# The indexer's second products on 128 rows instead of 64, with zeros in the other half, in a hybrid encoder step

## The chip, the core and the metric

The kernel runs on one core of a Trainium2 chip. The metric is the device time of one execution in microseconds (us); less is better. The engines are PE (TensorE: the products, with PEld for its weight loads), DVE (VectorE), ACT (ScalarE), POOL (GpSimd) and SP (SyncE, which here only issues transfers).

## The reference, cut to what matters

One layer mixes 512 prompt tokens and 64 sample tokens with a gated DeltaNet branch and a sparse attention branch. The sparse attention first needs a score for each pair of query and key, from 16 indexer heads of 64 dimensions that share one set of keys, and keeps the best keys of each query:

```python
dots = jnp.einsum('bthd,bsd->bths', qi.astype(jnp.float32), KI.astype(jnp.float32))
score = jnp.einsum('bth,bths->bts', wi.astype(jnp.float32), jax.nn.relu(dots))
visible = (k_pos[None, :] // CHUNK) <= (q_pos[:, None] // CHUNK)
score = jnp.where(visible[None], score, -jnp.inf)
top_val, top_idx = lax.top_k(score, topk)
```

For the prompt the keys are those of the prompt itself (512), for the sample they are 1024 cached ones and 64 new ones.

## The kernel before

**Products in parts.** Nearly all matrix products are made in the type fp32r, with each factor written as a first part (its rounding to fp32r) and a second part (what is left). A product is the sum of three: first by first, first by second, second by first. For the weight products these are the names `hh`, `hl` (the two parts of the input) and `whi`, `wlo` (the two parts of a weight tile).

**The stream of weight tiles.** `run_tile` takes one tile of 128 output columns after another: 96 products of 128 rows by 288 columns, first the 64 with `whi`, then the 32 with `wlo`. Within a tile it has ACT split the next tile's weights (hook 4, 14, 24, 34) and SP load a later one (hook 84). Everything else is made by small generators, called tasks. After each product `self.tick()` steps the tasks whose due time has come by a planner's own clock, and so each engine's instructions get one fixed order when the program is built.

**The scores.** Eight tiles of the stream, `qi0` to `qi7`, give the indexer's queries, two heads each. `qi_epi` writes for each of the two heads `s` a tile `qi[:, s, :]` of 128 rows: the head's first part in one half of the rows (rows 0 to 63 for s = 0, rows 64 to 127 for s = 1) and its second part in the other half. The keys' first part stands twice in `kih`, in both halves of the rows, and the keys' second part twice in `kil`. So one product of `qi` with `kih` over all 128 rows gives first by first and second by first at once, and a second product gives first by second from the 64 rows that hold the query's first part alone. `score` makes, for each of the two heads, three such pairs for the query blocks t = 3, 2, 1 (with 512, 384 and 256 keys), and then three units for the sample, each of three products with all 128 rows (`qss` with `kih`, `kih` and `kil`, 364 or 362 keys). Here a unit is what goes into one PSUM tile `dot`: two products for the prompt, three for the sample. There are two `dot` banks; ACT takes each unit out with a Relu (`relu`), and DVE adds it to the score (`msk`, `msks`).

**Where this lies.** `misc` splits the keys when its weight tile is done, `cache_idx` does so for the cached keys, and `run` allots `kih`, `kil` and zeroes the two `qss` tiles. The units of one pair of heads lie among the next weight tile's products. When the eighth pair is done, the choice of the best keys runs on DVE, and the stream goes on with the next weight tiles.

Of the kernel before, what the change touches and what calls it, by code (L numbers as in the profile page):

```python
# [7 lines left out]
F32 = mybir.dt.float32  # L8
F32R = mybir.dt.float32r
I32 = mybir.dt.int32  # L10
AF = mybir.ActivationFunctionType
ALU = mybir.AluOpType
# [6 lines left out]
TP = 512  # L19
# [186 lines left out]
class Kern(Plan):  # L206
# [446 lines left out]
    def misc(self):  # L653
        i, o, p, A, V, G, mT = self.i, self.o, self.p1, self.A, self.V, self.G, self.mT
# [3 lines left out]
        for a, b, at in ((0, TP, 0), (TP, T, TP + PAST)):  # L658
            c = slice(at, at + b - a)
            A.activation(self.kih[0:64, c], mT[0:64, a:b], AF.Copy)  # L660
            A.activation(self.kih[64:128, c], mT[0:64, a:b], AF.Copy)
            for R in (slice(0, 64), slice(64, 128)):
                V.tensor_tensor(self.kil[R, c], mT[0:64, a:b], self.kih[0:64, c].bitcast(F32), op=ALU.subtract)
        mt = p.tile([128, 5, 112], F32, name="mt", bufs=1)
        G.memset(mt[64:128, 4, :], 0.0)
        pt = yield from self.tr("mtp")
# [25 lines left out]
        x = p.tile(sh, F32, name="sx", bufs=1)  # L692
# [104 lines left out]
    def qi_epi(self, m):  # L797
        def epi(ps, s):
# [7 lines left out]
            halves = slice(0, 64), slice(64, 128)  # L806
            for b, R in enumerate(halves):
                A.activation(q[R, b, c], ps[R, :n], AF.Copy)
                V.tensor_tensor(q[halves[1 - b], b, c], ps[R, :n], q[R, b, c].bitcast(F32), op=ALU.subtract)
            if s:  # L810
                qs = self.qss[m % 2]
                for R in halves:
                    self.two(ps[R, 224:288], qs[R, 0, R], qs[R, 1, R])
# [3 lines left out]
    def score(self, m, qi, qs):  # L817
        p, A = self.p1, self.A
        accs, acs = self.msk, self.msks
        if m:  # L820
            yield from self.wait(self.score_tasks[m - 1])
        else:
            yield from self.wait(self.misc_task, self.cache_task)
        units = []
        for s in range(2):
            R = slice(64 * s, 64 * s + 64)
            for t in (3, 2, 1):
                nk = 128 * t + 128
                q, k = qi[:, s, 128 * t:128 * t + 128], slice(0, nk)
                units.append((((q, self.kih[:, k]), (q[R], self.kil[R, k])), nk, accs[t],  # L830
                              self.wi[:, t, 2 * m + s:2 * m + s + 1], m == 0 and s == 0))
        for a, n in ((0, 364), (364, 362), (726, 362)):
            kh, kl = (k[:, TP + a:TP + a + n] for k in (self.kih, self.kil))
            units.append((((qs[:, 0, :], kh), (qs[:, 1, :], kh), (qs[:, 0, :], kl)), n, acs[:, a:a + n],
                          self.wis[:, m:m + 1], m == 0))
        yield [qi, qs]
        last = []
        for n, (parts, w, acc, sc, first) in enumerate(units):
            if len(last) >= 2:
                yield [last[-2]]  # L840
            pd = yield from self.tp(f"dot{m}_{n}")
            for x, (q, k) in enumerate(parts):
                self.mm(pd[:, :w], q, k, start=x == 0, stop=x == len(parts) - 1)
            r = p.tile([128, 512], F32, tag="relu", name=f"relu{m}_{n}")
            A.activation(r[:, :w], pd[:, :w], AF.Relu)
            if first:
                self.V.tensor_scalar(acc, r[:, :w], sc, None, op0=ALU.mult)
            else:
                self.V.scalar_tensor_tensor(acc, r[:, :w], sc, acc, op0=ALU.mult, op1=ALU.add)
            last.append(r)  # L850
        if m == 7:
            yield from self.topk_all()
            self.topk_task = self.spawn(self.topks())
# [935 lines left out]
    def run(self):  # L1789
        tc = self.tc  # L1790
        with ExitStack() as ctx:
            ctx.enter_context(tc.manual_schedule())
            self.consts(ctx)
            cp = self.cp
            self.wi = cp.tile([128, 4, 16], F32, name="wi")
            self.wis = cp.tile([128, 8], F32, name="wis")
            for n in ("beta", "gc", "egc", "kds"):
                setattr(self, n, cp.tile([128, 5, 16], F32, name=n))
            self.gate = cp.tile([128, KO, 2], F32, name="gate")
            self.diag = cp.tile([128, 64], F32, name="diag")  # L1800
            self.heads, self.att, self.kvT, self.tok = {}, {}, {}, {}
            self.score_tasks, self.topk_task = [], None
            self.topk_gap, self.solve_gap, self.gada_gap = 100, 0, 5000
            self.plan()
            self.hctx = ExitStack()
            pss = self.start(ctx, self.hctx)
            self.catt, self.ap = self.pool("att", bufs=1)
            self.msk = [self.ap.tile([128, 128 * t + 128], F32, name=f"msk{t}") for t in range(4)]
            self.msks = self.ap.tile([128, NS], F32, name="msks")
            self.c1, self.p1 = self.pool("p1")  # L1810
            self.gpool, self.p2 = lambda: self.p1, None
            p = self.p1
            self.kih, self.kil = (p.tile([128, TP + NS], F32R, name=n, bufs=1) for n in ("kih", "kil"))
            self.qss = []
            for b in range(2):
                q = p.tile([128, 2, 128], F32R, name=f"qss{b}", bufs=1)
                self.V.tensor_scalar(q, self.ident.unsqueeze(1).to_broadcast([128, 2, 128]), 0.0, None, op0=ALU.mult)
                self.qss.append(q)
            self.tri = p.tile([128, 2, 128], F32, name="tri", bufs=1)
            self.cache_task = self.spawn(self.cache_idx())  # L1820
            self.load(3)
            for n in range(2):
                for s in range(2):
                    self.stream[n]["epi"](pss[2 * n + s], s)
            self.S.dma_start(self.tri, self.i["k_tri"])
            self.load(4)
            for n in range(2, len(self.stream) - 2):
                self.run_tile(n)
            self.run_last(n + 1)
            self.drain()  # L1830
            for _ in self.finish((2, 3, 4)):
                pass
            for c in (self.c8, self.c6, self.cmg, ):
                c.close()
# [57 lines left out]
```

## Time and profile before

| what | value |
|---|---|
| time, median of 3 runs | 3108.05 us (3101.53 to 3108.31) |
| the profiled execution: its time | 3106.55 us |
| its span, first to last instruction | 3104.8 us |
| PE busy | 2972.8 us, 96% of the span |
| DVE, ACT, POOL busy | 1389.1, 1542.5, 390.0 us |
| first and last product of the scores (`dot`) | 189.4 us, 328.2 us |

The time of an execution is the span and some 1.75 us around it. An engine's products are pipelined: a product's row shows how long it is in the engine, and the distance from its start to the next one's start shows what it costs when products follow each other without a pause. The granted clock of PE is given as a share of 2.4 GHz (0.5 is 1.2 GHz).

### The profile page before, as it was taken

What the parts mean: (1) busy time and instruction counts of PE and PEld (TensorE: products, weight loads), DVE (VectorE), ACT (ScalarE), POOL (GpSimd) and SP (SyncE); (2) the same over time, 40 slices, a digit from 0 to 9 for tenths busy, and PEclk for the clock granted to TensorE, in tenths of its full rate; (3) what the DMA queues carried; (4) which work ended last, traced back from release to release, by engine and by line L of the source; (5) the groups of instructions that cost most, each with busy time, mean ns of one, the idle gap of its engine ahead of it and who ended that gap; (6) DMA issues with size and microseconds to landing.
All of it is one profiled execution on the core that took longest, in us unless ns stands there. A gap on an engine that the chain in (4) does not pass through costs nothing.

```text
span 3104.8 us, 56419 instructions
## 1 busy us (share of the span) xinstructions
PE 2972.8 (96%) x22363; PEld 2816.3 (91%) x22363; DVE 1389.1 (45%) x4057; ACT 1542.5 (50%) x3332; POOL 390.0 (13%) x727
## 2 busy tenths in 40 slices
PE   6999999999999999999998799999999899999997
PEld 2588999999989989999998699999999899999897
DVE  3334899566667657765651244334422111111112
ACT  3255444555555556665653345444544444444454
POOL 1010111111111111111110000101101111111110
PEclk8999999999999999999999899999999999999999
DMA  9865787766666666676767767776769899888875
GB/s 325 270 147 114 171 185 175 159 162 161 154 144 145 150 145 146 145 167 136 165 153 159 163 160 168 188 177 158 175 148 248 227 234 232 213 209 214 225 159 141
DMA packets 567242, 552.40 MB, mean 178 GB/s; under 512 B 53505, under 2 KB 466066, under 8 KB 565762
## 3 DMA queue, kind: packets, MB, share of 16 engines
q1 hardware_dynamic: 512690, 351.58, 40.1%
q0 software_dynamic: 54144, 197.16, 33.5%
q8 instruction: 176, 2.88, 0.4%
q14 instruction: 88, 0.72, 0.1%
q10 hardware_dynamic: 144, 0.07, 0.0%
HBM read 303.54 MB, written 48.04 MB: 113 GB/s over the span
## 4 chain that ended last, share of the span: by engine, by line
PE 49%; DMA 9%; SPq 3%; ACT 2%; DVE 2%; issue 1%; POOL 0%; ACTq 0%; DVEq 0%; POOLq 0%
PE mm L218 41%; SPq L55 3%; DMA gbl<-d_gb 2%; DMA za<-d_za 2%; DMA wlo<-wraw 2%; PE ob L218 1%; PE lg L218 1%; DMA xf<-in_x_sample 1%; ACT wlo L55 1%; ACT whi L55 1%; PE po L218 1%; PE pT L233 1%; PE obs L218 1%; PE lgs L218 0%; DVE M L55 0%
## 5 line engine op out<-in xcount | busy, mean ns | idle before, releaser
L218 PE MATMUL mm<-hh,whi 128*128 128x288 f32 (+1 forms) x4448 | 1222.3, 301 | 6.1 <-ACT gth L55 5.8
L218 PE MATMUL mm<-hl,whi 128*128 128x288 f32 (+1 forms) x4448 | 1219.8, 300 | 0.0
L218 PEld LDWEIGHTS mm<-hh,whi 128*128 128x128 f32 (+1 forms) x4448 | 839.1, 189 | 22.0 <-issue 9.2
L218 PEld LDWEIGHTS mm<-hl,whi 128*128 128x128 f32 (+1 forms) x4448 | 839.4, 189 | 13.0 <-issue 9.1
L218 PE MATMUL mm<-hh,wlo 128*128 128x288 f32 (+1 forms) x4448 | 685.0, 303 | 4.9 <-DMA wlo<-wraw 4.9
L218 PEld LDWEIGHTS mm<-hh,wlo 128*128 128x128 f32 (+1 forms) x4448 | 619.5, 191 | 13.2 <-DMA wlo<-wraw 5.1
L55 POOL DMA_DIRECT2D wlo<-wraw x376 | 324.3, 863 | 2340.4 <-ACT wlo L55 2062.9
L55 ACT ACTIVATE whi<-wraw 128x512 fp32r<-128x512 f32 x756 | 467.3, 619 | 96.1 <-DMA wraw<-in_w_branch_b 40.2
L55 ACT ACTIVATE wlo<-whi 128x512 fp32r<-128x512 f32 x752 | 475.2, 632 | 70.0 <-PE mm L218 31.6
L55 DVE TENSOR_TENSOR Mt<-M 18x30 f32<-18x30 f32 (+14 forms) x480 | 151.8, 316 | 34.1 <-DMA M<-dN 24.8
L55 DVE TENSOR_TENSOR M<-M,Mt 18x30 f32<-18x30 f32 (+14 forms) x480 | 153.6, 320 | 16.5
L218 PE MATMUL mm<-ga,whi 128*128 128x288 f32 x1024 | 141.1, 297 | 7.1 <-DVE ta L55 6.4
L218 PEld LDWEIGHTS mm<-ga,whi 128*128 128x128 f32 x1024 | 138.3, 190 | 8.2 <-DVE ta L55 7.4
L218 PE MATMUL mm<-mg,whi 128*128 128x288 f32 x1024 | 144.3, 298 | 0.0
L218 PEld LDWEIGHTS mm<-mg,whi 128*128 128x128 f32 x1024 | 139.0, 190 | 0.0
L218 PE MATMUL mm<-gb,whi 128*128 128x288 f32 x1024 | 138.1, 294 | 0.0
L218 PEld LDWEIGHTS mm<-gb,whi 128*128 128x128 f32 x1024 | 136.5, 188 | 0.0
L55 DVE SCALAR_TENSOR_TENSOR cv<-raw,cw,cv 128x579 f32<-128x579 f32 x144 | 117.4, 815 | 4.3 <-ACT cv L55 0.8
L55 DVE SCALAR_TENSOR_TENSOR gacc<-gada,cs,gacc 128x512 f32<-128x512 f32 x120 | 86.6, 744 | 31.1 <-DMA gada<-in_w_ada 31.1
L55 ACT ACTIVATE x<-px 128x128 f32<-128x128 f32 (+1 forms) x80 | 21.9, 274 | 153.4 <-PE px L218 153.4
L55 ACT ACTIVATE raw<-mm 128x288 f32<-128x288 f32 x96 | 36.7, 382 | 99.3 <-PE mm L218 98.4
L55 DVE TENSOR_TENSOR xf<-yp,xf 128x512 f32<-128x512 f32 (+1 forms) x18 | 11.4, 632 | 161.1 <-PE yp L233 134.5
(476 smaller groups left out, 3310.7 us busy)
## 6 DMA issues: line engine op xcount, KB each, us to landing
wlo<-wraw POOLq DMA_DIRECT2D x376, 512.0 KB, 5.4
wraw<-in_w_in SPq DMA_DIRECT2D x140, 1024.0 KB
wa<-in_w_ada SPq DMA_DIRECT2D x64, 512.0 KB
gada<-in_w_ada SPq DMA_DIRECT2D x64, 256.0 KB
wraw<-in_w_branch_a SPq DMA_DIRECT2D x16, 1024.0 KB
wraw<-in_w_branch_b SPq DMA_DIRECT2D x16, 1024.0 KB
wraw<-in_w_out SPq DMA_DIRECT2D x16, 1024.0 KB
d_t<-gth SPq DMA_DIRECT2D x32, 288.0 KB
```

Of the source, the lines that this page charges most:

```text
L55: r = f(*a, **k)
L218: self.nc.tensor.matmul(out, lhsT, rhs, start=start, stop=stop, **k)
L233: self.nc.tensor.transpose(out, in_, self.ident[:k, :k])
```

## The change

A new tile `kiz` of 128 rows, 2 x 512, holds the second parts of the 512 prompt keys once for each `s`: in `kiz[:, 0, :]` they stand in rows 0 to 63 and rows 64 to 127 are zero, and in `kiz[:, 1, :]` they stand in rows 64 to 127 and rows 0 to 63 are zero. `run` writes the zeros with two DVE operations; `misc` writes the second parts there instead of into `kil`. The second product of a prompt unit then takes all 128 rows of `qi` against `kiz`, where it took 64 rows of `qi` against 64 rows of `kil`. The query's second part meets zeros. `kil` is still used for the sample.

```diff
@@ misc
-            for R in (slice(0, 64), slice(64, 128)):
-                V.tensor_tensor(self.kil[R, c], mT[0:64, a:b], self.kih[0:64, c].bitcast(F32), op=ALU.subtract)
+            for x, R in enumerate((slice(0, 64), slice(64, 128))):
+                V.tensor_tensor(self.kil[R, c] if at else self.kiz[R, x, :], mT[0:64, a:b], self.kih[0:64, c].bitcast(F32), op=ALU.subtract)
@@ score
         for s in range(2):
-            R = slice(64 * s, 64 * s + 64)
             for t in (3, 2, 1):
                 nk = 128 * t + 128
                 q, k = qi[:, s, 128 * t:128 * t + 128], slice(0, nk)
-                units.append((((q, self.kih[:, k]), (q[R], self.kil[R, k])), nk, accs[t],
+                units.append((((q, self.kih[:, k]), (q, self.kiz[:, s, k])), nk, accs[t],
                               self.wi[:, t, 2 * m + s:2 * m + s + 1], m == 0 and s == 0))
@@ run
+            self.kiz = p.tile([128, 2, TP], F32R, name="kiz", bufs=1)
+            for x, R in enumerate((slice(64, 128), slice(0, 64))):
+                self.V.tensor_scalar(self.kiz[R, x, :].rearrange("p (a b) -> p a b", b=128),
+                                     self.ident[R].unsqueeze(1).to_broadcast([64, 4, 128]), 0.0, None, op0=ALU.mult)
```

On PE the rows stand in the same order as before from the first to the last. This is the start of the first pair of heads, before the change (each row: line, operation, output and inputs, the output's partitions and columns):

```order
L218 MATMUL dot_0_0_1485<-kih,qi_1352 128x512
L218 MATMUL dot_0_0_1485<-kil,qi_1352 128x512
L218 MATMUL dot_1_0_1491<-kih,qi_1352 128x384
L218 MATMUL dot_1_0_1491<-kil,qi_1352 128x384
L218 MATMUL mm_1_1453<-hh,whi_1209 128x288
L218 MATMUL mm_1_1453<-hl,whi_1209 128x288
```

And this is the same place after it:

```order
L218 MATMUL dot_0_0_1488<-kih,qi_1355 128x512
L218 MATMUL dot_0_0_1488<-kiz,qi_1355 128x512
L218 MATMUL dot_1_0_1494<-kih,qi_1355 128x384
L218 MATMUL dot_1_0_1494<-kiz,qi_1355 128x384
L218 MATMUL mm_1_1456<-hh,whi_1212 128x288
L218 MATMUL mm_1_1456<-hl,whi_1212 128x288
```

Nothing moved; in 48 of PE's rows `kil` became `kiz`. ACT, POOL and SP have the same rows in the same order, too. On DVE two rows come in at the end of the start-up, before the first tokens of the keys are copied. Before:

```order
L55 TENSOR_TENSOR wlo_995<-wraw_898,whi_994 128x448 x4
L55 TENSOR_SCALAR qss_1033<-ident 128x256
L55 TENSOR_SCALAR qss_1035<-ident 128x256
L55 COPY tokk<-kvpk_0_1067 128x4x128
L55 COPY tokk<-kvqk_0_1073 64x128
L55 COPY tokk<-kvpk_0_1091 128x4x128
```

After:

```order
L55 TENSOR_TENSOR wlo_995<-wraw_898,whi_994 128x448 x4
L55 TENSOR_SCALAR kiz<-ident 64x512 x2
L55 TENSOR_SCALAR qss_1036<-ident 128x256
L55 TENSOR_SCALAR qss_1038<-ident 128x256
L55 COPY tokk<-kvpk_0_1070 128x4x128
L55 COPY tokk<-kvqk_0_1076 64x128
L55 COPY tokk<-kvpk_0_1094 128x4x128
```

The first `kiz` row also waits for two transfers' semaphores, where the first `qss` row waited for one of the two: these tiles take memory that tiles of the start-up held before.

## Rows read from the trace of the kernel before

**Rows 1.** The page, part 1: busy us of each engine, share, instructions.
```profile
PE 2972.8 (96%) x22363; PEld 2816.3 (91%) x22363; DVE 1389.1 (45%) x4057; ACT 1542.5 (50%) x3332; POOL 390.0 (13%) x727
```

**Rows 2.** By stretch: busy us of PE, PEld, DVE, ACT, POOL, clock, DMA, GB/s.
```profile
188.50:329.00 140.50, 140.50 (x871) 121.81 (x870) 56.50 (x113) 80.65 (x170) 12.68 (x15) 1.00 0.52 111
329.00:500.00 171.00, 171.00 (x1306) 170.45 (x1305) 158.54 (x319) 83.09 (x156) 26.59 (x51) 1.00 0.79 182
...
1655.00:1745.00 90.00, 58.60 (x358) 53.88 (x358) 17.41 (x57) 23.57 (x56) 5.17 (x6) 0.77 0.82 166
```

**Rows 3.** The tile `dot`: durations in ns, minimum/median/maximum, first and last start.
```profile
L218 PE MATMUL dot<-kih,qi x48: 276/364/447, 189.4 to 324.8; 128*128 128x512 f32 x16, 128*128 128x384 f32 x16, 128*128 128x256 f32 x16
...
L218 PE MATMUL dot<-kil,qi x48: 380/438/498, 189.8 to 325.0; 64*128 64x512 f32 x16, 64*128 64x384 f32 x16, 64*128 64x256 f32 x16
```

**Rows 4.** Timeline of PE: start, duration, what; the second pair's units.
```profile
203.61 0.39 PE L218 MATMUL dot<-kih,qi 128*128 128x512 f32 x1
203.93 0.50 PE L218 MATMUL dot<-kil,qi 64*128 64x512 f32 x1
204.36 0.45 PE L218 MATMUL dot<-kih,qi 128*128 128x384 f32 x1
...
205.10 0.40 PE L218 MATMUL mm<-hh,whi 128*128 128x288 f32 x1
205.34 0.30 PE L218 MATMUL mm<-hl,whi 128*128 128x288 f32 x1
...
208.39 0.28 PE L218 MATMUL dot<-kih,qi 128*128 128x256 f32 x1
...
209.15 0.30 PE L218 MATMUL mm<-hl,whi 128*128 128x288 f32 x1
```

**Rows 5.** Timeline of PE: the sample's units, and a run of 128-row weight products.
```profile
214.02 0.49 PE L218 MATMUL dot<-kih,qss 128*128 128x364 f32 x2
214.36 0.33 PE L218 MATMUL dot<-kil,qss 128*128 128x364 f32 x1
214.52 0.30 PE L218 MATMUL mm<-hh,wlo 128*128 128x288 f32 x1
...
340.19 4.40 PE L218 MATMUL mm<-hh,wlo 128*128 128x288 f32 x32
344.43 0.29 PE L218 MATMUL mm<-hh,whi 128*128 128x288 f32 x1
```

**Rows 6.** One whole tile of the score stage, by stretch (columns as in rows 2).
```profile
222.16:240.84 18.68, 18.68 (x120) 16.35 (x119) 7.55 (x15) 10.93 (x24) 1.72 (x2) 1.00 0.52 112
```

**Rows 7.** Timeline of PE: other products of 64 rows, in the DeltaNet stage.
```profile
704.70 0.29 PE L218 MATMUL mm<-hl,whi 128*128 128x288 f32 x1
704.93 0.68 PE L218 MATMUL y<-TT,e 64*64 64x64 f32 x8
705.53 0.40 PE L218 MATMUL mm<-hh,whi 128*128 128x288 f32 x1
705.77 0.29 PE L218 MATMUL mm<-hl,whi 128*128 128x288 f32 x1
```

**Rows 8.** Timeline of DVE at the end of the start-up, with the idle time before.
```profile
149.98 0.49 DVE L55 TENSOR_SCALAR qss<-ident 128x256 fp32r<-128x256 f32 x2
151.33 0.69 DVE L55 COPY tokk<-kvpk 128x512 f32<-128x512 f32 x1 [0.86 <-PE kvpk L233]
...
153.32 0.69 DVE L55 COPY tokk<-kvpk 128x512 f32<-128x512 f32 x1 [1.12 <-PE kvpk L233]
```

**Rows 9.** Timeline of ACT in the second pair.
```profile
206.66 0.98 ACT L55 ACTIVATE relu<-dot 128x512 f32<-128x512 f32 x2
...
210.27 0.60 ACT L55 ACTIVATE relu<-dot 128x512 f32<-128x512 f32 x1 [0.87 <-PE dot L218]
```

**Rows 10.** PE's waits over the whole span: in total, times, longest.
```profile
PE lg L218 <- DVE L L55: 18.0, 4, 17.5
...
PE mm L218 <- DMA wlo<-wraw: 4.9, 1, 4.9
```

## The prediction

> **What bounds the kernel now.** I read the page first, then the stretches, then the changed place. The page says that PE is busy for 96% of the span, DVE and ACT for half of it or less [rows 1]. By stretch PE has no gap at all from 188.5 to 500 us, at the full granted clock [rows 2]: 140.50 of 140.50 us in the stretch with the scores, 171.00 of 171.00 us in the next. In the score stretch ACT is busy for 80.65 us, DVE for 56.50 us and the transfers for 0.52 of the time. So there PE alone sets the pace, and what a product there costs PE is paid in full. PE's gaps elsewhere add up to 3104.8 - 2972.8 = 132 us; the most of them in one place is in 1655 to 1745 us, where it is busy for 58.60 of 90 us.
>
> The tile `dot` shows an oddity [rows 3]. The product with `kil` has the same columns as the one with `kih` just before it and half its rows, but is longer: a median of 438 against 364 ns.
>
> The timeline says more, if the starts are read [rows 4]. After the 64-row product of 512 columns at 203.93 the next product starts 0.43 us later; after the 128-row one at 203.61 it is 0.32 us. And the first weight product behind a 64-row product holds up its successor as well: 205.10 to 205.34 is 0.24 us. Where all products have 128 rows none of this is there [rows 5]: the sample's three products of 364 columns, one of them with `kil`, go from 214.02 to 214.52, 0.167 us each, and 32 weight products go from 340.19 to 344.43, 0.1325 us each. The DeltaNet stage shows the same marks around its own 64-row products [rows 7]: 0.23 us from 704.70 to the first of them, and again 0.24 us from 705.53 to 705.77, between two weight products. So what costs is the passage from 128 rows to 64 and back, paid three times: on the way in, on the way out, and at the product after that.
>
> **The change, part by part.**
>
> *48 products go from 64 rows to 128* (8 pairs of heads, 6 units each). What does a unit cost if all its products have 128 rows? From 0.1325 us at 288 columns and 0.167 us at 364 the step is 0.45 ns a column, so some 0.234 us at 512 columns, 0.176 us at 384 and 0.118 us at 256. Now the units of rows 4, from the start of a unit to the second weight product behind it. The 512 and 384 units together take 203.61 to 205.34, 1.73 us; with 128 rows 2 x 0.234 + 2 x 0.176 + 0.1325 = 0.95 us; 0.78 us saved. The 256 unit takes 208.39 to 209.15, 0.76 us; with 128 rows 0.24 + 0.13 = 0.37 us; 0.39 us saved. That is 0.39 us a unit, and 48 x 0.39 = 18.7 us.
>
> A second way to it goes by a whole tile [rows 6]: 18.68 us, less 96 weight products at 0.1325 us (12.72 us) and 9 sample products at 0.167 us (1.50 us), leaves 4.46 us for 12 prompt products. At 128 rows these would be 4 x (0.234 + 0.176 + 0.118) = 2.11 us; 2.35 us saved a tile, 18.8 us in eight. I take 18.7 us. No row shows a product with `kiz`; its nearest row is the sample's product with `kil` on 128 rows, which has everything in common with it but the number of columns. The low bound comes from the durations alone: if only a product's own length shrank, 438 to 364 ns, it would be 48 x 0.074 = 3.6 us.
>
> *Weight loads.* There are as many as before, and with 128 rows instead of 64. Loads keep PEld busy for 16.35 us of a tile's 18.68 [rows 6], and those of 128 rows hold nothing up in rows 5. No cost.
>
> *Two DVE operations that write zeros.* The nearest row is `qss`, 128 x 256, two in 0.49 us [rows 8]. With half the rows and twice the columns I take 0.5 us each, the upper end; the lower is 0.25 us, if the time goes by the elements. DVE idles for 0.86 us just there, so two at 0.5 us push the `tokk` copy at 151.33 back by some 0.14 us. The second copy from `kvpk` begins at 153.32 us after another wait of 1.12 us, so the slip ends there, and PE has its weight products meanwhile. Cost 0; without this cover 1 us, once. The added wait for a transfer's semaphore is for memory that the start-up used, and these loads have been consumed by then: 0; its price otherwise is a rival below.
>
> *The keys' second parts* are written by the same two DVE operations of 64 x 512 to another address: 0.
>
> *Relu and the banks.* Units now follow each other faster, and the third unit needs the bank of the first. In the second pair the two Relus begin at 206.66 and end at 207.64, and the first, 512 columns, takes some 0.60 us like the one at 210.27, so it ends at 207.26 [rows 9]; they come 2 us behind their products, so ACT and not PE sets them, and I let them stay where they are. The third unit starts at 208.39 [rows 4], 1.13 us later, and comes 0.78 us earlier after the change. The bank is still free 0.35 us ahead. Cost 0; should the Relu be late by all of 0.78 us it would be 0.43 us a tile, 7 x 0.43 = 3 us (the first pair has no such hold).
>
> *Behind the scores.* The choice of the best keys and the next weight tiles start from the last score, so both move up together, and PE is without a gap up to 500 us [rows 2]. PE's largest wait, 17.5 us for `L` [rows 10], is for work that starts from earlier products of the stream, so it moves along. Two things may change its size and that of the smaller ones: transfers that meet at another moment, and the granted clock, which falls to 1.2 GHz where PE has waited (a mean of 0.77 in 1655 to 1745 us [rows 2]). There the lost clock is 90 x 0.23 = 20.7 us; a third more or less of it is 7 us, as much as the three runs of before differ by (6.8 us). I take 0 and keep 7 us on either side.
>
> *The sum*, against the profiled execution: 3106.55 - 18.7 = 3087.9 us. The median of before is 1.5 us above that execution, so I predict 3089 us, 0.6% less.
>
> **The rivals.** A difference of 0.3%, 9.3 us, is about what a measurement of this kernel can tell from none.
>
> *The rows don't matter.* The long steps might come from using the same columns of `qi` twice, or from the two heads' tiles; then all stays as it is, at 3108 us. Against it: `hh` and `hl` also use the same `whi` columns twice in a row, 32 times in a tile, and the tile's sum [rows 6] comes out with all of these at 0.1325 us; and rows 7 show the marks with other tiles. 4 in 100. The Trainium skill, "TensorE: Matmul & The Clock Gate", section "Why this matters for your kernels", says that a single product of few rows takes the time of a full one, and that small ones gain only where several run at once in their own row groups. By that alone 64 or 128 rows cost the same and the change would bring 0; the trace agrees in that half the rows are not faster, but it shows the passage as well, and no two 64-row products side by side here that the change could part.
>
> *Part is lost behind.* The stage shrinks by 18.7 us, but half or more comes back as longer waits in 1655 to 1745 us, such as that at `L`, if what PE waits for there is paced by the transfers instead of by PE. For it: in that stretch the DMA share is 0.82 [rows 2]. Against it: weights made PE wait just once, for 4.9 us [rows 10]. That gives 3097 to 3106 us. 7 in 100.
>
> *Slower.* The first zeroing waits for a transfer that has not landed. DVE then stands, the `tokk` copies behind it do too, PE's next transposes, the ones that are copied at 153.32 us, lack a bank, and every product behind them waits. To eat the gain DVE must stand until about 172 us, and until 181 us to show as slower; at 190 us it would be 3108 + 190 - 153 - 18.7, some 3126 us. Nothing in rows 8 speaks for a load in flight on that memory. 2 in 100.
>
> **How the numbers follow.** The forecast has 87 in 100: 18.7 us with 7 us of clock and waits on either side and up to 3 us for the banks, 3082 to 3099 us. The low bound of the product term, 3.6 us, would be 3104 us; the sample's rows speak so plainly for starts without a pause that it goes with the 4 in 100 of the first rival. The range 3080 to 3099 us holds the forecast and a little of the partial loss, and leaves out less than 2 in 10. Below 3098.7 us counts as faster: 0.88, the forecast and the best of the partial loss; within 9.3 us: 0.10; slower: 0.02.
>
> **What the profile after would show.** Right: products `dot` with `kiz` of 128 rows, as long as those with `kih`; starts 0.23, 0.17 and 0.12 us behind them at 512, 384 and 256 columns; 0.13 us at the weight product behind; a tile of scores in 16.3 instead of 18.7 us; the last `dot` product at about 309.5 us instead of 328.2; PE without a gap there; the waits of rows 10 at about their size. Wrong: PE waiting for `relu` ahead of a third unit, the `kiz` zeroing beginning late, long steps that stay at 128 rows, or a gain at 310 us that is gone by 1750 us.

## The result and the profile after

The changed kernel takes 3086.59 us, the median of 11 runs (3076.14 to 3097.69); the kernel before, in 11 runs beside them, takes 3106.55 us (3097.32 to 3109.93). The ratio is 0.9936, with a 95% interval from 0.9922 to 0.9950: 20 us less, where 18.7 us were forecast. The profiled execution after the change is the fastest of the 11, with a span of 3074.4 us.

The page's busy times after the change, to be held against [rows 1]:

```profile
PE 2949.8 (96%) x22363; PEld 2811.9 (91%) x22363; DVE 1389.5 (45%) x4059; ACT 1542.1 (50%) x3332; POOL 390.6 (13%) x727
```

PE has lost 23 us of busy time at the same number of instructions, and DVE has two instructions more. By stretch, with the columns of [rows 2]: the scores, the stage behind them, the stage with PE's largest wait, and one whole tile of scores, which answers to [rows 6]:

```profile
185.60:307.20 121.60, 121.60 (x871) 120.28 (x870) 55.71 (x113) 79.05 (x170) 12.77 (x15) 1.00 0.58 126
307.20:478.00 170.80, 170.80 (x1306) 170.25 (x1305) 158.52 (x319) 83.28 (x156) 27.06 (x51) 1.00 0.80 184
1631.00:1718.00 87.00, 56.88 (x335) 51.86 (x334) 16.75 (x54) 23.32 (x56) 5.17 (x6) 0.78 0.82 167
214.59:230.90 16.31, 16.31 (x120) 16.15 (x119) 7.45 (x15) 10.73 (x24) 1.72 (x2) 1.00 0.58 129
```

A tile takes 16.31 us where it took 18.68. PE is still without a gap and at the full clock, and the same 871 products stand in a stretch that is 18.9 us shorter. DVE and ACT do the same work in it. The weight loads show best what has gone: PEld was busy for 16.35 us of a tile's 18.68, and is now busy for 16.15 us of 16.31, so loads and products follow each other with hardly a hole. The view of PEld shows where the holes were. Before the change, at the place of [rows 4], the load for the product at 203.93 begins at 203.93, and that for the one at 204.36 at 204.36:

```profile
203.93 0.18 PEld L218 LDWEIGHTS dot<-kil,qi 64*128 64x128 f32 x1 [0.26 <-issue]
204.36 0.19 PEld L218 LDWEIGHTS dot<-kih,qi 128*128 128x128 f32 x1 [0.25 <-issue]
```

After the change the load for the product at 198.64 begins at 198.41, together with the product before:

```profile
198.41 0.19 PEld L218 LDWEIGHTS dot<-kiz,qi 128*128 128x128 f32 x1
198.64 0.19 PEld L218 LDWEIGHTS dot<-kih,qi 128*128 128x128 f32 x1
```

So it is at all 48 of the 64-row products, on the way in and on the way out: the load begins 2 ns ahead of its product, where elsewhere in this stage it begins a median of 130 ns ahead. Weights are loaded ahead from one 128-row product to the next, then, and not from 128 rows to 64 or back. Why they are not is not shown.

The products themselves, in the view of the tile `dot`, and the timeline of PE in the second pair, which answer to [rows 3, 4]:

```profile
L218 PE MATMUL dot<-kih,qi x48: 280/338/397, 186.6 to 303.4; 128*128 128x512 f32 x16, 128*128 128x384 f32 x16, 128*128 128x256 f32 x16
...
L218 PE MATMUL dot<-kiz,qi x48: 279/335/395, 186.8 to 303.5; 128*128 128x512 f32 x16, 128*128 128x384 f32 x16, 128*128 128x256 f32 x16
```

```profile
198.41 0.39 PE L218 MATMUL dot<-kih,qi 128*128 128x512 f32 x1
198.64 0.39 PE L218 MATMUL dot<-kiz,qi 128*128 128x512 f32 x1
198.87 0.34 PE L218 MATMUL dot<-kih,qi 128*128 128x384 f32 x1
199.04 0.34 PE L218 MATMUL dot<-kiz,qi 128*128 128x384 f32 x1
199.22 0.29 PE L218 MATMUL mm<-hh,whi 128*128 128x288 f32 x1
199.35 0.29 PE L218 MATMUL mm<-hl,whi 128*128 128x288 f32 x1
...
202.38 0.28 PE L218 MATMUL dot<-kih,qi 128*128 128x256 f32 x1
202.50 0.28 PE L218 MATMUL dot<-kiz,qi 128*128 128x256 f32 x1
202.62 0.30 PE L218 MATMUL mm<-hh,whi 128*128 128x288 f32 x1
202.75 0.29 PE L218 MATMUL mm<-hl,whi 128*128 128x288 f32 x1
```

Read the starts. The steps at 512, 384 and 256 columns are 0.23, 0.17 to 0.18 and 0.12 us, and the weight product behind takes its usual 0.13 us. The stretch from 198.41 to 199.35 is 0.94 us, where the same rows took 1.73 us, and that from 202.38 to 202.75 is 0.37 us, where it was 0.76. Note that the median of the products with `kih` fell, too, from 364 to 338 ns, though nothing in them was changed. That is the work of eight of the 48, those of 384 columns right behind a 64-row product, which went from 0.45 us to 0.34; the others kept their length.

The two zeroings on DVE, which answer to [rows 8]; the second row has no idle time ahead of it any more:

```profile
147.10 0.86 DVE L55 TENSOR_SCALAR kiz<-ident 64x512 fp32r<-64x512 f32 x2
...
148.34 0.69 DVE L55 COPY tokk<-kvpk 128x512 f32<-128x512 f32 x1
...
150.35 0.69 DVE L55 COPY tokk<-kvpk 128x512 f32<-128x512 f32 x1 [1.13 <-PE kvpk L233]
```

ACT's first two Relus of the second pair, as in [rows 9], and PE's waits, as in [rows 10]:

```profile
201.47 0.98 ACT L55 ACTIVATE relu<-dot 128x512 f32<-128x512 f32 x2
```

```profile
PE lg L218 <- DVE L L55: 17.6, 4, 17.1
...
PE mm L218 <- DMA wlo<-wraw: 4.8, 1, 4.8
```

The largest wait moved along and kept its size. The first and last products of the scores started at 189.4 and 328.2 us before and at 186.6 and 306.4 us after. So of the 30.4 us by which this one span is shorter, 18.9 lie in the score stage; 2.9 us were there already before it, in the start-up, and 8.6 us came behind it. Of these, 5.4 us lie around one place, where `px` waits for `r`: 4.2 us before, 1.8 us after, and the clock fell before and did not fall after:

```profile
1434.00:1450.00 16.00, 12.04 (x77) 10.57 (x78) 8.00 (x34) 2.16 (x6) 0.00 (x0) 0.79 0.31 76
```

```profile
1406.00:1422.00 16.00, 14.19 (x115) 12.65 (x115) 8.44 (x35) 3.63 (x11) 1.19 (x4) 1.00 0.63 136
```

In two later profiles of the changed kernel (e6 and e9 below) the clock fell there as it did before, to a mean of 0.79 over 16 us. The span of e6 is 19.7 us shorter than that of before, nearly all of it in the score stage. So I don't count the 11.5 us outside the stage as the change's; no run separates them from it.

### The profile page after: what moved, and what is told of

It is laid out like the page before. It is cut to its first block, busy times and chain, and to the rows that moved or that the text cites. A ratio compares the mean times of both kernels' runs of the same rounds, so it can differ in the third digit from the quotient of the medians.

```text
span 3074.4 us, 56422 instructions
## 1 busy us (share of the span) xinstructions
PE 2949.8 (96%) x22363; PEld 2811.9 (91%) x22363; DVE 1389.5 (45%) x4059; ACT 1542.1 (50%) x3332; POOL 390.6 (13%) x727
## 4 chain that ended last, share of the span: by engine, by line
PE 78%; DMA 11%; SPq 3%; ACT 3%; DVE 3%; issue 2%; POOL 0%; ACTq 0%; DVEq 0%; POOLq 0%
PE mm L218 63%; SPq L55 3%; DMA za<-d_za 2%; DMA wlo<-wraw 2%; DMA gbl<-d_gb 1%; PE ada L218 1%; PE ob L218 1%; DMA wa<-in_w_ada 1%; PE lg L218 1%; PE po L218 1%; PE dot L218 1%; ACT wlo L55 1%; PE mmp L218 1%; DMA xf<-in_x_sample 1%; ACT whi L55 1%
## 5 line engine op out<-in xcount | busy, mean ns | idle before, releaser
L218 PEld LDWEIGHTS mm<-hh,wlo 128*128 128x128 f32 (+1 forms) x4448 | 618.2, 191 | 11.5 <-DMA wlo<-wraw 5.1
```

What stands on the lines that cost most here:

```text
L218: self.nc.tensor.matmul(out, lhsT, rhs, start=start, stop=stop, **k)
```

## The experiments

**e1: the same tile, 64 rows.** The first question is which part of the change counts, the rows or the new tile.

```diff
-                q, k = qi[:, s, 128 * t:128 * t + 128], slice(0, nk)
-                units.append((((q, self.kih[:, k]), (q, self.kiz[:, s, k])), nk, accs[t],
+                q, k, R = qi[:, s, 128 * t:128 * t + 128], slice(0, nk), slice(64 * s, 64 * s + 64)
+                units.append((((q, self.kih[:, k]), (q[R], self.kiz[R, s, k])), nk, accs[t],
```

> The changed kernel with its tile kiz and the two zeroing operations, but the second prompt products take only the 64 rows that hold keys, as before the change. Passage theory (the cost is in going from 128 rows to 64 and back): all long steps return, 0.43 us behind a 64-row product of 512 columns and 0.24 us at the weight product behind it; a score tile takes 18.7 us; the time is that of before, ratio 0.997 to 1.003. Rival (the gain came from the other tile, its address, or the zeroed memory): steps as after, a score tile of 16.3 us, ratio 0.994.

Measured: 3104.28 us, ratio 0.9995 (0.9981 to 1.0008). PE's timeline in the second pair:

```profile
203.04 0.50 PE L218 MATMUL dot<-kiz,qi 64*128 64x512 f32 x1
203.47 0.45 PE L218 MATMUL dot<-kih,qi 128*128 128x384 f32 x1
...
204.21 0.40 PE L218 MATMUL mm<-hh,whi 128*128 128x288 f32 x1
204.45 0.30 PE L218 MATMUL mm<-hl,whi 128*128 128x288 f32 x1
```

0.43 us behind the 64-row product and 0.24 us at the weight product are back, and a tile's 120 products take 18.68 us again:

```profile
221.40:240.08 18.68, 18.68 (x120) 16.35 (x118) 7.55 (x15) 10.94 (x23) 1.72 (x2) 1.00 0.51 112
```

With the new tile, its address and its zeroing in place the whole gain is gone, so it is in the rows alone.

**e4: no zeros at all.** The other way round: 128 rows without `kiz`. The prompt's scores lack the keys' second parts here.

```diff
-                units.append((((q, self.kih[:, k]), (q[R], self.kil[R, k])), nk, accs[t],
+                units.append((((q, self.kih[:, k]), (q, self.kih[:, k])), nk, accs[t],
```

> The kernel before, with a second 128-row product with kih in place of the 64-row product with kil for the prompt; there is no kiz and no zeroing. It leaves the keys' second parts out of the prompt's scores. Passage theory: the same steps as after the change, 0.23, 0.18 and 0.12 us at 512, 384 and 256 columns, a score tile of 16.3 us, ratio 0.992 to 0.996. If the zeros in kiz or the zeroing operations had a price or a gain of their own, this would differ from the changed kernel by it: over 3 us in the score stage would show.

Measured: 3081.06 us, ratio 0.9916 (0.9896 to 0.9937). One tile of scores by stretch:

```profile
215.93:232.24 16.31, 16.31 (x120) 16.15 (x119) 7.46 (x15) 10.71 (x24) 1.72 (x2) 1.00 0.59 129
```

The tile takes the 16.31 us of the changed kernel, with the same busy times of PE and its weight loads and the other engines within 0.02 us, so the zeros cost nothing in this stage. The ratio lies 0.002 below that of the changed kernel and just under the range that was expected; the two intervals overlap, and the score stage is as long in both, 119.8 us.

**e2 and e2b: by product or by passage?** The prediction put the cost to the passage between 128 and 64 rows. It could as well belong to each 64-row product. These two kernels change the number of the one and keep the number of the other. In e2 each 64-row product is cut in two:

```diff
+                if len(parts) == 2 and x == 1:
+                    for c in (slice(0, w // 2), slice(w // 2, w)):
+                        self.nc.tensor.matmul(pd[:, c], q, k[:, c], start=False, stop=c.stop == w)
+                    self.account_pe(pd, [q, k], max(107, w / 2.4 + 3))
+                    continue
                 self.mm(pd[:, :w], q, k, start=x == 0, stop=x == len(parts) - 1)
```

> The kernel before, with each 64-row product cut into two 64-row products of half the columns; rows, order and planner's account as before. Passage theory: as many passages as before, so only the floor of one more product is added, 0.01 to 0.1 us a unit, 0.5 to 5 us in 48 units; the second half starts 0.12 to 0.13 us behind the first at 512 columns. Rival (each 64-row product costs by itself, for instance because its weights are not loaded ahead): the excess doubles, another 0.2 to 0.39 us a unit, 10 to 19 us, ratio 1.003 to 1.006.

In e2b one unit of each pair has its products in the other order, so that two 64-row products meet:

```diff
-                units.append((((q, self.kih[:, k]), (q[R], self.kil[R, k])), nk, accs[t],
+                parts = ((q, self.kih[:, k]), (q[R], self.kil[R, k]))
+                units.append((parts[::-1] if t == 2 and s == 0 else parts, nk, accs[t],
```

> The kernel before, with the two products of the unit s = 0, t = 2 swapped, so that in each pair of heads the 64-row products of the first two units stand back to back. Passage theory: one passage less in each of eight tiles; the stretch from the first unit's start to the second weight product behind the second unit takes 1.34 instead of 1.73 us, 3 us in all, too little for one time. Rival (cost by product): 1.73 us as before.

Measured: e2 takes 3109.20 us, ratio 1.0010 (0.9996 to 1.0023); e2b, one run, 3107.20 us. The first two units in e2's timeline, 96 products of 64 rows where there were 48:

```profile
225.36 0.39 PE L218 MATMUL dot<-kih,qi 128*128 128x512 f32 x1
225.68 0.50 PE L845 MATMUL dot<-kil,qi 64*128 64x256 f32 x2
226.11 0.44 PE L218 MATMUL dot<-kih,qi 128*128 128x384 f32 x1
226.47 0.47 PE L845 MATMUL dot<-kil,qi 64*128 64x192 f32 x2
226.87 0.40 PE L218 MATMUL mm<-hh,whi 128*128 128x288 f32 x1
227.11 0.29 PE L218 MATMUL mm<-hl,whi 128*128 128x288 f32 x1
```

From 225.36 to 227.11 is 1.75 us, where it was 1.73 us with half as many 64-row products [rows 4]. One part of the expectation was wrong: the second half starts 0.22 us behind the first, not 0.12 to 0.13, as its own row shows:

```profile
225.90 0.28 PE L845 MATMUL dot<-kil,qi 64*128 64x256 f32 x1
```

The same two units in e2b:

```profile
222.82 0.39 PE L218 MATMUL dot<-kih,qi 128*128 128x512 f32 x1
223.14 0.67 PE L218 MATMUL dot<-kil,qi 64*128 64x512 f32 x2
223.75 0.44 PE L218 MATMUL dot<-kih,qi 128*128 128x384 f32 x1
224.03 0.29 PE L218 MATMUL mm<-hh,whi 128*128 128x288 f32 x1
224.16 0.29 PE L218 MATMUL mm<-hl,whi 128*128 128x288 f32 x1
```

1.34 us, as the passage theory had it: the columns are those of before, and one passage is gone. The score stage, from the first `dot` product's start to the last one's, takes 138.8 us before, 140.1 us in e2 and 135.6 us in e2b. Both sides of the comparison say the same: a passage there and back costs 0.39 us whether one or two 64-row products stand in it. e2's interval excludes what the cost by product would give.

The single starts also divide the price. In e2 a step at 256 columns should be 0.12 us; the first half takes 0.22 us to the second, and the second 0.21 us to the 128-row product. In e2b the second 64-row product has a row of its own as well:

```profile
223.49 0.33 PE L218 MATMUL dot<-kil,qi 64*128 64x384 f32 x1
```

From 223.14 to it are 0.34 us, where a 128-row step takes 0.23, and from it to 223.75 are 0.26 us, where it takes 0.17 to 0.18. So each passage, in and out alike, adds some 0.09 us ahead of the first product beyond it and some 0.10 us ahead of the one that follows, and two passages make the 0.39 us.

**e5: the same in the DeltaNet stage.** If the passage is what costs, it can be saved at other places. The sample has 64 tokens, and so each of the 16 DeltaNet heads has three such places: `px`, `pS` with `po`, and the transpose `oTq`. Here they get 128 rows, with zeros that POOL writes (core of the edit):

```diff
+        G.memset(ot[64:128, 4, :], 0.0)
+        G.memset(kd[64:128, 4, :], 0.0)
...
-            self.mm(px[:n, :128], TT[:n, b:b + n], r)
+            self.mm(px[:n, :128], TT[:, b:b + n], r)
...
-            self.mm(pS[:, :128], kd[:n, c, :], x[:n])
-            self.mm(po[:n, :128], QK[:n, b:b + n], x[:n], start=Sc is None)
+            self.mm(pS[:, :128], kd[:, c, :], x)
+            self.mm(po[:n, :128], QK[:, b:b + n], x, start=Sc is None)
...
-        self.T32(pt[:, :64], ot[:64, 4, :])
+        self.nc.tensor.transpose(pt[:, :128], ot[:, 4, :], self.ident)
```

For these chunks `x` and `r` are two tiles whose upper rows are zeroed once, and `TT` has its own rows zeroed for each head.

> The changed kernel, and besides 48 places of the DeltaNet stage go from 64 rows to 128: for the sample's 64 tokens the products px, pS and po (zeros in the upper half of their inputs) and the transposes oTq, in each of 16 heads. Order on PE and SP as after the change; POOL gets some 50 more memsets. Passage theory: from a weight product to the second one behind, in the changed kernel's trace, px costs 0.33 us more with 64 rows than with 128, pS with po 0.52 us, oTq some 0.37 us; 16 x 1.22 = 19.5 us less than the changed kernel, if PE is the bound there too, so about 3067 us and a ratio to before of 0.987. Rival (in the DeltaNet stage PE waits for the solve's chain anyway, and the memsets stand in POOL's way): little or nothing comes through, ratio to before 0.992 to 0.995.

> The changed kernel once more, on the same chip as its neighbour, for the comparison with it and because the executions after the change spread over 20 us. Passage theory: 3082 to 3090 us median, ratio to before 0.992 to 0.995, the score stage from first to last dot 119.8 us whatever the time of the whole. Rival (the gain depends on the execution): the score stage itself varies by several us.

Measured: e5 takes 3077.44 us, ratio 0.9906 (0.9885 to 0.9927); the changed kernel beside it, e6, 3091.04 us, ratio 0.9945 (0.9925 to 0.9965). Better than the change by 13.6 us of medians, and not by the 19.5 us expected. I measured each place as in the expectation, from the start of the last weight product ahead to that of the second one behind, less 0.266 us for two weight products, as the median over the heads. `oTq` went from 0.48 to 0.19 us, `pS` with `po` from 0.97 to 0.79 us, where the chunks of 128 tokens take 0.45 us; `px` stayed at 0.56 us. That makes 16 x (0.29 + 0.18) = 7.5 us. The intervals allow this as well as 13.6 us; where the rest would come from is not shown. So the expectation was wrong about `px` and half wrong about `po`. These two have not only 64 rows, but also 64 columns of weights, and the columns were left at 64. The same holds of the 64-row products in [rows 7], which therefore could not tell rows from columns.

In e6 the score stage takes 119.8 us as in the profile after, at a span 10.7 us longer, and 119.8 us in e9: the gain in the stage does not vary, the rest of the execution does. The median of e6 lies 1 us above the range expected for it, its ratio within.

**e7 to e9: the columns, too.** In e7 `px` and `po` take 64 neighbouring columns of their weights along; the wanted results then come out on the upper 64 partitions, and the results of the others aren't read (the edit is shown against e5).

```diff
-            self.mm(px[:n, :128], TT[:, b:b + n], r)
+            self.mm(px[:, :128], TT[:, b - e:b + n], r, m=n)
...
-            A.activation(x[:n], px[:n, :128], AF.Copy)
+            A.activation(x[:n], px[e:e + n, :128], AF.Copy)
```

Here `e` is 64 for the sample's chunk and 0 for the others; both products of `po` are treated in the same way, and `m` keeps the planner's account as it was, so that the order is that of e5.

> The kernel of e5, and the sample's px and both products of po also have 128 columns of weights instead of 64 (64 neighbouring columns go along and their results are not read). Order as in e5. Passage theory, widened to columns: px goes from 0.56 us beyond its two weight products to the 0.22 us of the other chunks, and pS with po from 0.79 to 0.45 us; with oTq that is 16 x (0.33 + 0.52 + 0.29) = 18 us less than the changed kernel, 10.7 us less than e5; ratio to before 0.986 to 0.989. Rival (rows alone matter, and px is long for another reason): both stay as in e5, ratio as its neighbour's.

> The kernel of e5 once more, beside e7 on the same chip: rows padded to 128, columns of px and po still 64. Both theories: ratio to before 0.988 to 0.992, px 0.56 us and pS with po 0.79 us beyond their weight products.

> The changed kernel on the same chip as e7 and e8. Both theories: ratio to before 0.992 to 0.996; the passage theory puts it 7 us above e8 (rows) and 18 us above e7 (rows and columns).

Measured: e7 3064.52 us, ratio 0.9865 (0.9843 to 0.9887); e8 3076.46 us, 0.9906 (0.9886 to 0.9926); e9 3089.03 us, 0.9938 (0.9917 to 0.9959). The timeline of PE around the third head's `px` for the sample, in the changed kernel (64 rows, 64 columns):

```profile
700.06 0.29 PE L218 MATMUL mm<-hl,whi 128*128 128x288 f32 x1
700.28 0.43 PE L218 MATMUL px<-r,TT 64*64 64x128 f32 x2
700.64 0.40 PE L218 MATMUL mm<-hh,whi 128*128 128x288 f32 x1
700.88 0.29 PE L218 MATMUL mm<-hl,whi 128*128 128x288 f32 x1
```

In e8 (128 rows, 64 columns):

```profile
708.04 0.29 PE L218 MATMUL mm<-hl,whi 128*128 128x288 f32 x1
708.26 0.43 PE L218 MATMUL px<-xr,TT 128*64 128x128 f32 x2
708.62 0.40 PE L218 MATMUL mm<-hh,whi 128*128 128x288 f32 x1
708.86 0.29 PE L218 MATMUL mm<-hl,whi 128*128 128x288 f32 x1
```

And in e7 (128 rows, 128 columns):

```profile
703.56 0.29 PE L218 MATMUL mm<-hl,whi 128*128 128x288 f32 x1
703.70 0.38 PE L218 MATMUL px<-xr,TT 128*128 128x128 f32 x2
703.84 0.38 PE L218 MATMUL mm<-hh,whi 128*128 128x288 f32 x1
704.05 0.29 PE L218 MATMUL mm<-hl,whi 128*128 128x288 f32 x1
```

0.82 us with 64 of both, 0.82 us with 128 rows alone, 0.49 us with 128 of both. For `px` padding the rows is worth nothing while the columns stay at 64, and the prompt's products before the change, with 64 rows and 128 columns, paid for their rows. `pS` with `po` went from 0.79 to 0.45 us, as expected. The first product of `po` gained nothing: it stands behind `pks`, which still has 64 columns, and the two together kept their 0.78 us in all these kernels, where the chunks of 128 tokens take 0.45. By ratios e7 lies 0.0073 below the changed kernel of the same chip, some 22.7 us of 3104, and e8 0.0032, some 9.9 us; expected were 18 and 7, and the intervals reach 0.002, some 6 us, to either side of each. e7 is the fastest version here, 1.35% below the kernel before.

## Why the prediction was right

The change did what the sum says, for the reason that it gives.

*PE sets the pace, so the stage's cost is paid in full.* Right: the stretch lost 18.9 us with the same work in it, and PE has no gap in it before or after.

*The cost is in the passage.* Right, and shown: e1 takes the rows back and loses all, e4 gets all without a zero, e2 doubles the 64-row products at next to no cost, e2b takes a passage out and gains just its price. The rival that the rows don't matter is excluded by e1 and e4. Two things in the prediction were too coarse. The price is not paid three times but four, twice at each passage: the 0.43 us on the way out hold the second part of the way in. And the passage is not one of rows only, since `px` paid as much at 128 rows and 64 columns; the change kept 128 columns throughout, so the sum did not feel it.

*The size.* The steps that were worked out from the sample's and the weight products, 0.234, 0.176 and 0.118 us, came out at 0.23, 0.17 to 0.18 and 0.12 us. The tile saves 18.68 - 16.31 = 2.37 us against 2.35 us, eight of them 19.0 us. The Trainium skill, "TensorEngine Tiling (Array Packing)", section "Tiling Modes", says under its key properties that a change of the tiling mode drains the engine. The trace agrees in part: at a passage the next weights are not loaded ahead, and a row overlaps the next one by 0.07 us (203.61 and 0.39, then 203.93) instead of 0.16 (198.41 and 0.39, then 198.64); these ends are modelled, so a full drain is not shown.

*The zeroing.* Cost 0, right: two operations took 0.86 us, so 0.43 us each and not 0.5. The idle time ahead of the first `kvpk` copy took them in, and the second copy still waits 1.13 us for PE. The added wait shows as nothing.

*The banks.* Right, and close: the Relus begin at 201.47 us, so the first should end at about 202.07 us, and the third unit starts at 202.38. That is 0.3 us of room, where 0.35 us was forecast from 1.13 us.

*Behind the scores.* The wait for `L` came along at 17.1 us, and nothing of the gain was given back: three comparisons give 0.9936, 0.9945 and 0.9938. The 7 us on either side for clock and waits was rather small for one execution: the 11 runs after the change spread over 21.6 us, those of before over 12.6.

*What would show it.* All the signs of "right" are there but for one number: the last `dot` product started at 306.4 us, not at 309.5 us, since the profiled execution was 2.9 us ahead before the stage began. That was luck of the execution and no part of the forecast.

The slower rival needed a load still in flight when the zeroing was due; it began at 147.10 us with no idle time ahead of it. The rival of a partial loss is not seen in any of the three comparisons.

## What to carry to other kernels

Among back-to-back products of full size look for products with fewer rows or fewer columns of weights, and read the starts, not the durations: the price stands at the product itself, at the next one and at the one after that. If a lone product of half the rows can be had with full rows and zeros from an idle engine, it was worth some 0.3 to 0.4 us here where PE set the pace. Rows and columns of weights must both be full, and so must those of the neighbours: the first product of `po` gained nothing behind `pks`. Several partial products that must stay are better put side by side, as e2b shows for two.

## What the runs showed of the hardware that was not expected

A product with 128 rows and 64 columns of weights paid as much as one with 64 and 64: `px` takes 0.82 us in both forms and 0.49 us only at 128 by 128. This does not hold of transposes: `kdq`, with 128 rows and 64 columns of weights, takes 0.19 us in the kernel before, measured like the places of e5 and as the median of nine, which is what `oTq` takes at 128 by 128; with 64 rows `oTq` took 0.48 us.

Within one passage a second 64-row product is not dear, but its step is no faster than that of a 128-row one either. In e2b the two of 512 and 384 columns take 0.61 us from the first one's start to the next 128-row product, where their 128-row counterparts after the change take 0.23 + 0.18 = 0.41 us by their steps; the 0.20 us between are the two surcharges that e2 shows, 0.10 and 0.09 us.
